# A two-layer decoder trunk: which use of a mixer weight stores its high part, and where small constants are loaded

## The chip, the cores and the metric

The kernel runs on one core of a Trainium2 chip. The metric is the time of one execution on the device in microseconds; lower is better. The engines are TensorE (PE; its weight loads are listed as PEld), VectorE (DVE), ScalarE (ACT), GpSimd (POOL) and SyncE (SP), which issues the transfers; 16 DMA engines carry them between DRAM and the on-chip memory.

## The reference

A trunk of two layers runs over 1040 tokens (16 meta tokens and 1024 real ones) of width 1024. In each layer a mixer projects the normalised input, attends in three ways (sliding window, stick breaking, gated linear) and projects back; a PEER feed-forward network then picks 16 of 4096 experts for each of eight heads. Cut to what matters:

```python
for i in range(DEPTH):                                  # DEPTH = 2
    h = h + hybrid_mixer(rms_norm(h, attn_norm[i]), w_in[i], ..., w_out[i])
    h = h + peer_ffn(rms_norm(h, ffn_norm[i]), peer_w_q[i], peer_sub_keys[i], peer_u[i], peer_v[i])
return rms_norm(h[:, BLOCK:], final_norm)

def hybrid_mixer(xn, w_in, ..., w_out):
    proj = xn @ w_in                                    # 1024 x 2320
    ...                                                 # three kinds of attention
    return mixed @ w_out                                # 1024 x 1024
```

## The kernel before

**Numbers in two parts.** Matrix products in float32 are made from numbers cut into a high and a low part: TensorE multiplies high by high, high by low and low by high. For a weight, `wload` brings a piece of 128x512 floats (256 KB) into one of four raw buffers, and `split` writes the high part with ScalarE (line 274) and the low part as raw minus high, here half on GpSimd and half on VectorE (line 281).

**Quarters.** The mixer takes the tokens in four quarters (272, 256, 256 and 256 tokens). For each quarter `proj_span` makes 18 groups of `dense` (36 pieces of `w_in`, called `a0_...` and `a1_...` for the two layers), attention follows, and `out_span` makes 8 groups of `dense` (16 pieces of `w_out`, `o0_...`, `o1_...`). All matmuls of `dense` are line 335: 12 for each piece. So each piece of a mixer weight is used four times in its layer, once for each quarter.

**Kept parts.** At the first use of a piece `wpiece` splits the raw weights and `keep` (line 293) writes the parts to DRAM. Mixer weights ask for both parts (`both=True`), other weights for the low one alone. A later use finds the name in `kept` and loads the low part (line 311), and the high part either from DRAM (line 310) or, where it was not kept, by loading the raw piece and making the high part anew with one ScalarE copy (line 308). The parts land in two rings of five buffers, `whi` and `wlo`, the raw pieces in the ring of four, `wraw`. The rings are handed out in program order. `make_m`, which builds a table for the feed-forward network between attention and projection, uses the `wraw` ring too: four pieces a call, three calls after the first quarter's attention.

**Order.** The program order is: normalise the first quarter, load the small constants (`load_constants`, seven transfers), load the second quarter's activations for their squares (`first(1)`, eight transfers), then project the first quarter. Within a layer the projection of quarter q+1 stands between the attention and the output projection of quarter q. A scheduler turns the program into one fixed list for each engine, by priority in program order and by its own estimate of when operands are ready, so attention of one quarter and the projection of the next lie interleaved. At run time each engine's list stays as it is. Engine tasks depend on each other by semaphores that the framework places.

In the second layer the first quarter is projected between the two halves of the first layer's last expert product (`values`, matmuls of line 1203).

Of the kernel before, what the change touches and what calls it, by code (L numbers as in the profile page):

```python
# [59 lines left out]
def tile_trunk(ctx, tc, h0, w_pk, wgate, w2, glab, w_out, wqT, keysT, u_pk, v_w, sinks,  # L60
# [104 lines left out]
    def ps1(tag="a"):  # L165
        r = rings[tag]
        r[1] += 1
        return banks[r[0][(r[1] - 1) % len(r[0])]]
# [57 lines left out]
    def load_constants():  # L226
        SP.dma_start(w2s[0:16], w2.rearrange("l r c -> r l c"))
        SP.dma_start(w2s[16:32], w2.rearrange("l r c -> r l c"))
        SP.dma_start(glab_sb, glab)
        SP.dma_start(g_mix, n_mix)  # L230
        SP.dma_start(sink_b, sinks.rearrange("l h -> (l h)").unsqueeze(0).to_broadcast([128, 16]).rearrange(
            "p (l h) -> p l h", l=DEPTH))
        SP.dma_start(g_ffn, n_ffn)
        SP.dma_start(g_fin, n_fin)
# [48 lines left out]
    def wload(src):  # L283
        raw = sb([128, 512], F32, "wraw")
        SP.dma_start(raw, src)
        return raw

    kept = {}

    def keep(name, part):  # L290

        t = dram.tile([128, 512], F32, name=name, tag=name)
        SP.dma_start(t, part.bitcast(F32))
        return t

    def wpiece(src, key=None, both=False):


        hi = sb([128, 512], F32R, "whi")
        lo = sb([128, 512], F32R, "wlo")  # L300
        if key not in kept:
            split(wload(src), hi, lo)
            if key is not None:
                kept[key] = (keep(f"{key}h", hi) if both else None, keep(f"{key}l", lo))
            return hi, lo
        kh, kl = kept[key]
        if kh is None:
            ACT.activation(hi, wload(src), AF.Copy)  # L308
        else:
            SP.dma_start(hi.bitcast(F32), kh)  # L310
        SP.dma_start(lo.bitcast(F32), kl)
        return hi, lo
# [26 lines left out]
    def rstd(ver, sp, sqk=None):  # L339

        acc = sqs[ver]
        ss = ps1("d")
        n = len(sp.tiles)
        if sqk:
            PE.matmul(ss[:, 0:8], zb, identb[:, 0:8], start=True, stop=False)
            for sq in sqk:
                for j, (o, m) in enumerate(sp.tiles):
                    PE.matmul(ss[0:m, j:j + 1], sq[:, o:o + m], ones[:, 0:1], start=False, stop=False)
            PE.matmul(ss[:, 0:8], zb, identb[:, 0:8], start=False, stop=True)
        else:  # L350
            for j, (o, m) in enumerate(sp.tiles):
                PE.matmul(ss[0:m, j:j + 1], acc[:, sp.c0 + o:sp.c0 + o + m], ones[:, 0:1], start=True, stop=True)
        ms = sb([128, 8], F32, "nms")
        rs = sb([128, 8], F32, "nrs")
        grp = [(0, 1, META), (1, n, 128)] if sp.meta else [(0, n, 128)]
        for a, b, m in grp:
            DVE.tensor_scalar(ms[0:m, a:b], ss[0:m, a:b], 1.0 / D, EPS, op0=ALU.mult, op1=ALU.add)
            POOL.tensor_tensor(rs[0:m, a:b], ms[0:m, a:b], mhalf[0:m, a:b], op=ALU.pow)
        ps = ps1("d")
        for j, (o, m) in enumerate(sp.tiles):  # L360
            PE.matmul(ps[:, o:o + m], rs[0:m, j:j + 1].to_broadcast([m, 128]), ident[0:m, 0:m], start=True, stop=True)
        rb = sb([128, 272], F32, "rb")
        ACT.activation(rb[:, 0:sp.w], ps[:, 0:sp.w], AF.Copy)
        return rb

    def apply(ver, sp, g, x, rb, ks=range(KT), src=None, buf="ht"):

        w = sp.w
        for k in ks:
            xt = sb([128, 272], F32, buf)  # L370
            if src is None:
                SP.dma_start(xt[:, 0:w], hv[ver][k][:, sp.c0:sp.c1])
            DVE.scalar_tensor_tensor(xt[:, 0:w], xt[:, 0:w] if src is None else src[:, k], g[:, k:k + 1], rb[:, 0:w],
                                     op0=ALU.mult, op1=ALU.mult)
            xh = x.at(0, k, 0, w)
            ACT.activation(xh, xt[:, 0:w], AF.Copy)
            DVE.tensor_tensor(x.at(1, k, 0, w), xt[:, 0:w], xh.bitcast(F32), op=ALU.subtract)
# [45 lines left out]
    def proj_span(l, L, sp, x):  # L423

        A = Layer()
        w = sp.w
        A.sp = sp
        A.mo = mo = META if sp.meta else 0
        A.b0 = b0 = (sp.c0 + mo - META) // 128
        def proj(g):  # L430
            return dense(w_pk[l, g], x, sp, f"a{l}_{g}")

        def vtrans(g, dst, col, base, pad):
            pss = proj(g)
            st = sb([128, 384], F32, "vst", 2)
            off = 0
            if pad:
                off = 112
                if sp.meta:
                    POOL.memset(st[:, 0:112], 0.0)  # L440
            evac(st[:, off:off + w], pss, sp)
            tp = ps1("d")
            for j in range(2):
                PE.transpose(tp[:, j * 128:(j + 1) * 128], st[:, off + mo + j * 128:off + mo + j * 128 + 128], ident)
            if sp.meta:
                if pad:
                    PE.transpose(tp[:, 256:384], st[:, 0:128], ident)
                    DVE.tensor_copy(dst[:, base - 1, col:col + 128], tp[:, 256:384])
                else:
                    PE.transpose(tp[0:16, 256:384], st[:, 0:16], ident)  # L450
                    DVE.tensor_copy(dst[0:16, 0, col:col + 128], tp[0:16, 256:384])
            DVE.tensor_copy(dst[:, base:base + 2, col:col + 128],
                            tp[:, 0:256].rearrange("p (b c) -> p b c", b=2))

        pr = str((b0 // 2) % 2)
        A.qaT = sb([128, 4, 272], F32, "qaT" + pr)
        A.qbT = sb([128, 2, 272], F32, "qbT" + pr)
        A.qcT = sb([128, 272], F32, "qcT" + pr)
        A.kcT = sb([128, 272], F32, "kcT" + pr)
        A.cum = cum = sb([128, 272], F32, "cum" + pr)  # L460
        A.gr = sb([128, 2, 272], F32, "gr" + pr)
        A.vc = sb([128, 3, 256], F32, "vc" + pr)
        for i in range(2):
            evac(L.kbT[:, i, sp.c0:sp.c1], proj(i), sp)
        for i in range(2):
            evac(A.qbT[:, i], proj(2 + i), sp, scale=0.125)
        for i in range(2):
            vtrans(4 + i, L.vb, 128 * i, b0 + 1, False)
        yield A
        if sp.meta:  # L470
            POOL.memset(L.kaT[:, slot(-1) * 128:slot(-1) * 128 + 112], 0.0)
        evac(L.kaT[:, slot(b0) * 128 - mo:slot(b0) * 128 - mo + w], proj(6), sp)
        vtrans(7, L.va, 0, slot(b0), True)
        for i in range(4):
            evac(A.qaT[:, i], proj(8 + i), sp, scale=0.125)
        evac(A.kcT, proj(12), sp)
        evac(A.qcT, proj(13), sp, scale=32.0 ** -0.5)

        graw = sb([128, KT, 16], F32, "graw")
        SP.dma_start(graw, wgate[l])  # L480
        ghl = sb([128, KT, 32], F32R, "ghl")
        ACT.activation(ghl[:, :, 0:16], graw, AF.Copy)
        DVE.tensor_tensor(ghl[:, :, 16:32], graw, ghl[:, :, 0:16].bitcast(F32), op=ALU.subtract)
        ps = ps1("d")
        for k in range(KT):
            PE.matmul(ps[0:32, 0:w], ghl[:, k, :], x.at(0, k, 0, w), start=(k == 0), stop=False)
            PE.matmul(ps[0:16, 0:w], ghl[:, k, 0:16], x.at(1, k, 0, w), start=False, stop=(k == KT - 1))
        A.gl = sb([32, 272], F32, "gl" + pr)
        ACT.activation(A.gl[:, 0:w], ps[0:32, 0:w], AF.Copy)
        for i in range(2):  # L490
            vtrans(14 + i, A.vc, 128 * i, 1, False)
        for i in range(2):
            pss = proj(16 + i)
            evac(A.gr[:, i], pss, sp)
        yield A
# [739 lines left out]
    quarters = [Span(0, 272), Span(272, 528), Span(528, 784), Span(784, 1040)]  # L1235
# [5 lines left out]
    XR = [Rows((HA, HB)), Rows((HC, HA)), Rows((HB, HC)), Rows((HA, HB))]  # L1241
# [14 lines left out]
        make_m(0, i)  # L1256
    L = attn_layer(0)
    apply(0, quarters[0], g_attn[:, 0], XR[0], rstd(0, quarters[0], sqk), src=hq)
    load_constants()
    first(1)  # L1260
    pr = proj_span(0, L, quarters[0], XR[0])
    A = next(pr)
    rb = rstd(0, quarters[1])
    apply(0, quarters[1], g_attn[:, 0], XR[1], rb, range(4))
    next(pr)
# [1 line left out]
    for l in range(DEPTH):  # L1267
# [10 lines left out]
        for q in range(4):  # L1278
# [25 lines left out]
            if q < 3:  # L1304
                A = nA
# [53 lines left out]
        if more:  # L1359
            values(l, Q, G, (0, 1), 0)  # L1360
            L = attn_layer(l + 1)
            pr = proj_span(l + 1, L, quarters[0], XR[0])
            A = next(pr)
# [80 lines left out]
```

## Time and profile before

| | |
|---|---|
| runs before, median (lowest to highest) | 3353.25 us (3343.89 to 3354.38), 3 runs |
| profiled execution, time | 3348.59 us |
| profiled execution, span | 3346.8 us |
| mean granted clock of TensorE | 0.959 |
| TensorE matmuls, busy | 3139.3 us, 94% |
| VectorE, ScalarE, GpSimd, busy | 62%, 39%, 29% |
| moved by DMA | 655.56 MB, 195 GB/s over the span |

The profile comes from one execution. Busy times are sums over instructions; a matmul's end is modelled, so a busy TensorE isn't TensorE at its peak, and the mean time of one matmul tells more. "Idle before, releaser" is the time in which an engine waited and what ended it. The granted clock is given as a share of full speed.

### The profile page before, as it was taken

The page shows a single profiled execution, that of the slowest core. Times are in us where ns is not written, and L with a number is a line of the kernel's source. Part 1 is how long each engine was busy: PE and PEld are TensorE (multiplying, and loading weights), DVE is VectorE, ACT ScalarE, POOL GpSimd, SP SyncE. Part 2 cuts the span into 40 slices and gives each one's busy share as a digit, 9 for nine tenths or more (in the row PEclk, how much of TensorE's full clock was granted, in tenths as well). Part 3 has the DMA queues.
Part 4 walks back from the last instruction along what each step waited for, and adds up shares of the span by engine and source line. Part 5 has one row for each costly group of instructions (what it writes and reads, how often), then busy time and mean ns, then how long its engine had stood idle before and what let it go on. Part 6 is the DMA issues. An engine that isn't in the chain of part 4 may idle for free.

```text
span 3346.8 us, 65733 instructions
## 1 busy us (share of the span) xinstructions
PE 3139.3 (94%) x23453; PEld 2636.6 (79%) x23453; DVE 2074.0 (62%) x6694; ACT 1311.1 (39%) x3013; POOL 958.4 (29%) x976
## 2 busy tenths in 40 slices
PE   7999999988999988999898999999889999899998
PEld 7686887768999987888874878877668888688788
DVE  4546446689885389753225464457796835986457
ACT  4534334424334343324344343344333344343354
POOL 4314021313454341010401131213244524301135
PEclk9899998989999999999997999999799999999999
DMA  8767774736346555446964677757454466554665
GB/s 292 235 194 251 248 258 136 215 127 236 128 137 191 182 174 172 157 145 200 333 232 141 211 263 241 251 161 238 149 181 148 154 191 219 172 179 143 195 191 169
DMA packets 406442, 655.56 MB, mean 196 GB/s; under 512 B 44560, under 2 KB 122464, under 8 KB 406112
## 3 DMA queue, kind: packets, MB, share of 16 engines
q1 hardware_dynamic: 406112, 651.35, 60.3%
q8 instruction: 184, 3.01, 0.4%
q14 instruction: 146, 1.20, 0.1%
HBM read 492.70 MB, written 158.47 MB: 195 GB/s over the span
## 4 chain that ended last, share of the span: by engine, by line
PE 67%; DVE 20%; DMA 7%; ACT 2%; issue 2%; SPq 1%; POOL 1%; DVEq 0%; POOLq 0%; ACTq 0%
PE b L1113 18%; PE b L1203 15%; PE b L335 13%; PE b L1164 4%; PE b L987 3%; PE b L703 2%; DVE arena_r L1197 2%; DMA arena<-h 2%; DVE arena L998 2%; DVE arena L1000 2%; DVE arena L997 2%; PE b L618 2%; PE b L757 2%; DMA arena<-in_w_pk_dram 1%; DVE arena L999 1%
## 5 line engine op out<-in xcount | busy, mean ns | idle before, releaser
L281 POOL TENSOR_TENSOR arena_r<-arena,arena_r 128x512 fp32r<-128x512 f32 (+1 forms) x440 | 555.4, 1268 | 869.5 <-ACT arena_r L274 800.3
L1113 PE MATMUL b<-arena_r 128*128 128x512 f32 (+2 forms) x3840 | 763.0, 357 | 17.5 <-DVE arena L261 15.5
L1203 PE MATMUL b<-arena_r 128*128 128x512 f32 (+2 forms) x4224 | 749.7, 337 | 31.4 <-DVE arena_r L1197 24.6
L1203 PEld LDWEIGHTS b<-arena_r 128*128 128x128 f32 x4224 | 643.8, 190 | 126.2 <-DVE arena_r L1197 35.7
L335 PE MATMUL b<-arena_r 128*128 128x256 f32 (+1 forms) x4992 | 702.6, 295 | 36.4 <-ACT arena_r L274 10.0
L1113 PEld LDWEIGHTS b<-arena_r 128*128 128x128 f32 x3840 | 626.0, 191 | 115.6 <-DVE arena L261 16.2
L335 PEld LDWEIGHTS b<-arena_r 128*128 128x128 f32 x4992 | 643.9, 196 | 76.3 <-issue 19.7
L274 ACT ACTIVATE arena_r<-arena 128x512 fp32r<-128x512 f32 x456 | 285.1, 629 | 479.8 <-PE b L1113 104.1
L1197 DVE TENSOR_TENSOR arena_r<-arena,arena_r 128x512 fp32r<-128x512 f32 (+2 forms) x352 | 270.8, 783 | 314.6 <-ACT arena_r L1196 313.5
L308 ACT ACTIVATE arena_r<-arena 128x512 fp32r<-128x512 f32 x288 | 181.2, 631 | 384.3 <-PE b L1203 120.9
L987 PE MATMUL b<-arena_r 128*128 128x256 f32 (+1 forms) x1632 | 208.9, 283 | 3.4 <-DMA arena_r<-m_3l 1.8
L987 PEld LDWEIGHTS b<-arena_r 128*128 128x128 f32 (+1 forms) x1632 | 196.5, 183 | 13.5 <-issue 4.4
L1152 DVE TENSOR_TENSOR arena<-arena 128x2048 f16<-128x2048 f16 x129 | 176.1, 1367 | 45.3 <-PE b L1164 45.3
L257 POOL TENSOR_TENSOR arena<-arena 128x256 f32<-128x256 f32 (+1 forms) x126 | 107.9, 856 | 315.1 <-ACT arena L256 312.4
L1120 POOL TENSOR_TENSOR arena<-arena 128x32 f32<-128x32 f32 (+25 forms) x91 | 98.5, 1089 | 305.4 <-ACT arena L1171 206.6
L1196 ACT ACTIVATE arena_r<-arena 128x512 fp32r<-128x512 f32 (+2 forms) x352 | 172.2, 502 | 31.1 <-PE b L1203 27.6
L1164 PEld LDWEIGHTS <-arena 128*128 128x128 f16 x4128 | 144.4, 118 | 17.2 <-issue 14.4
L1169 DVE SCALAR_TENSOR_TENSOR arena<-b,arena 128x224 f32<-128x224 f32 (+20 forms) x129 | 63.1, 499 | 145.9 <-PE b L1164 145.7
L1164 PE MATMUL b<-arena 128*128 128x32 f16 x4128 | 152.3, 190 | 0.0
L715 DVE TENSOR_TENSOR_SCAN arena<-arena,zf 128x384 f32<-128x384 f32 (+6 forms) x116 | 104.1, 900 | 76.5 <-ACT arena L710 75.5
L421 ACT ACTIVATE arena<-b 128x256 f32<-128x256 f32 (+1 forms) x144 | 55.2, 384 | 211.7 <-PE b L335 211.2
L1157 DVE TENSOR_TENSOR arena<-arena 128x1024 f16<-128x1024 f16 x129 | 123.3, 956 | 0.1
(267 smaller groups left out, 3796.7 us busy)
## 6 DMA issues: line engine op xcount, KB each, us to landing
arena<-in_v_w_dram SPq DMA_DIRECT2D x288, 256.0 KB, 2.9
arena<-in_u_pk_dram SPq DMA_DIRECT2D x256, 256.0 KB, 3.0
arena_r<-a_0h SPq DMA_DIRECT2D x108, 256.0 KB, 3.7
arena_r<-a_0l SPq DMA_DIRECT2D x108, 256.0 KB, 3.9
arena_r<-a_1h SPq DMA_DIRECT2D x108, 256.0 KB, 3.2
arena_r<-a_1l SPq DMA_DIRECT2D x108, 256.0 KB, 3.5
arena<-m SPq DMA_DIRECT2D x96, 256.0 KB, 4.5
arena<-h SPq DMA_DIRECT2D x192, 128.0 KB, 3.1
```

The costliest lines, as they stand in the source:

```text
L274: ACT.activation(hi, src, AF.Copy)
L281: e.tensor_tensor(lo[:, a:b], src[:, a:b], hi[:, a:b].bitcast(F32), op=ALU.subtract)
L308: ACT.activation(hi, wload(src), AF.Copy)
L335: PE.matmul(ps, wt[:, ks], x.at(low, k, xo, sp.w), start=(k == 0 and i == 0), stop=(k == KT - 1 and i == 2))
L987: PE.matmul(ps, yv(half, low, k, o, m), wt[:, kk * 256:kk * 256 + 256], start=(k == 0 and i == 0 and e == 0), stop=(k == KT - 1 and i == 2 ...
L1113: PE.matmul(ps, wt[:, ks], yv(h, low, k, 0, w // 2 if h is None else w), start=(k == 0 and i == 0), stop=(k == KT - 1 and i == 2))
L1152: DVE.tensor_tensor(Lh, iotaM.unsqueeze(1).to_broadcast([128, 4, 128, 4]), v4(P.mT[half], 128), op=ALU.is_equal)
L1157: DVE.tensor_tensor(R, R0.unsqueeze(2).to_broadcast([128, 4, 2, 32, 4]), P.gg[half][:, t0 // 4:t0 // 4 + 4].unsqueeze(3).to_broadcast([128 ...
L1164: PE.matmul(ps[:, i * 32:(i + 1) * 32], Lh[:, b, :, t], R[:, b, part, :, t], start=(part == 0), stop=(part == 1))
L1196: ACT.activation(ah, G[:, r, o:o + w], AF.Copy)
L1197: last = DVE.tensor_tensor(al, G[:, r, o:o + w], ah.bitcast(F32), op=ALU.subtract)
L1203: PE.matmul(ps, wt[:, d * 128:d * 128 + 128], pr[low], start=(opens and r == 0 and i == 0), stop=(closes and r == 31 and i == 2))
```

## The change

Of the two parts of a mixer weight only the low one is now written to DRAM at the first use. At the second use the raw piece is loaded again, its high part is made by a ScalarE copy and written to DRAM then; third and fourth use load both parts as before. Apart from that, the small constants and the second quarter's activations are now loaded after the first six groups of the first quarter's projection (`next(pr)` runs it up to its first `yield`) in program order, no longer ahead of them.

```diff
@@ wpiece
         if key not in kept:
             split(wload(src), hi, lo)
             if key is not None:
-                kept[key] = (keep(f"{key}h", hi) if both else None, keep(f"{key}l", lo))
+                kept[key] = [None, keep(f"{key}l", lo)]
             return hi, lo
         kh, kl = kept[key]
         if kh is None:
             ACT.activation(hi, wload(src), AF.Copy)
+            if both:
+                kept[key][0] = keep(f"{key}h", hi)
         else:
             SP.dma_start(hi.bitcast(F32), kh)
         SP.dma_start(lo.bitcast(F32), kl)
@@ the main program
     apply(0, quarters[0], g_attn[:, 0], XR[0], rstd(0, quarters[0], sqk), src=hq)
+    pr = proj_span(0, L, quarters[0], XR[0])
+    A = next(pr)
     load_constants()
     first(1)
-    pr = proj_span(0, L, quarters[0], XR[0])
-    A = next(pr)
     rb = rstd(0, quarters[1])
```

## Rows read from the trace of the kernel before

**Rows 1.** The page, busy time of the engines (first part).

```profile
PE 3139.3 (94%) x23453; PEld 2636.6 (79%) x23453; DVE 2074.0 (62%) x6694; ACT 1311.1 (39%) x3013; POOL 958.4 (29%) x976
```

**Rows 2.** Busy time by stretch; the first column after the colon is the length.

```profile
core 0: us, PE busy (x) PEld busy (x) DVE busy (x) ACT busy (x) POOL busy (x), PEclk, DMA share, GB/s
8.00:107.60 99.60, 82.00 (x533) 74.43 (x531) 47.80 (x128) 44.76 (x108) 41.97 (x62) 0.91 0.92 311
107.60:150.00 42.40, 38.32 (x236) 22.31 (x237) 23.58 (x72) 21.93 (x78) 17.49 (x19) 0.72 0.59 188
150.00:245.00 95.00, 94.66 (x760) 76.58 (x758) 45.47 (x109) 37.28 (x107) 14.79 (x20) 1.00 0.65 200
260.00:300.00 40.00, 36.95 (x294) 30.14 (x293) 26.10 (x57) 20.76 (x62) 21.14 (x21) 1.00 0.96 324
...
400.00:440.00 40.00, 39.51 (x307) 35.10 (x307) 22.15 (x63) 16.01 (x50) 7.97 (x9) 1.00 0.86 287
1604.00:1682.30 78.30, 66.82 (x471) 61.90 (x469) 20.60 (x46) 30.11 (x64) 37.94 (x40) 0.96 1.01 358
1670.00:1680.00 10.00, 8.92 (x66) 8.01 (x64) 2.66 (x8) 3.47 (x7) 3.76 (x4) 1.00 1.04 386
1682.30:1760.00 77.70, 77.17 (x331) 61.02 (x332) 22.39 (x35) 35.37 (x65) 2.67 (x19) 1.00 0.64 213
1840.00:1915.00 75.00, 73.51 (x594) 61.57 (x595) 30.58 (x72) 23.81 (x68) 8.56 (x12) 1.00 0.68 220
...
2068.00:2110.00 42.00, 41.51 (x324) 36.97 (x324) 23.48 (x67) 18.09 (x52) 7.58 (x8) 1.00 0.86 286
```

**Rows 3.** The same stretches, line 335 alone: PE, PEld, PEclk, DMA share, GB/s.

```profile
8.00:107.60 99.60, 65.23 (x411) 61.09 (x411) 0.91 0.92 311
107.60:150.00 42.40, 4.20 (x22) 3.44 (x22) 0.72 0.59 188
...
260.00:300.00 40.00, 23.30 (x165) 21.04 (x163) 1.00 0.96 324
363.00:375.00 12.00, 11.14 (x92) 10.98 (x93) 1.00 0.84 267
...
1604.00:1682.30 78.30, 58.31 (x414) 55.31 (x414) 0.96 1.01 358
```

**Rows 4.** What PE waited for, 8 to 110 us: total us, times, longest.

```profile
PE b L335 <- ACT arena_r L274: 3.3, 5, 1.4
PE b L335 <- POOL arena_r L281: 3.3, 4, 2.0
```

**Rows 5.** The same, 1590 to 1690 us.

```profile
PE b L335 <- ACT arena_r L274: 4.2, 2, 3.1
PE b L444 <- ACT arena L421: 3.8, 5, 1.7
PE b L335 <- POOL arena_r L281: 1.6, 4, 0.5
```

**Rows 6.** Busy time by stretch, line 274 on ScalarE alone.

```profile
8.00:107.60 99.60, 21.99 (x36) 0.91 0.92 311
```

**Rows 7.** Timeline of the start: start, length, engine, line, what, idle before.

```profile
5.03 0.43 SPq L227 DMA_DIRECT2D w2s<-in_w_dram  x1
...
8.35 1.85 SPq L285 DMA_DIRECT2D arena<-in_w_pk_dram  x4
...
14.33 3.30 DVE L281 TENSOR_TENSOR arena_r<-arena,arena_r 128x256 fp32r<-128x256 f32 x2 [1.16 <-ACT arena_r L274]
...
15.59 0.40 ACT L363 ACTIVATE arena<-b 128x272 f32<-128x272 f32 x1 [0.26 <-PE b L361]
...
17.75 1.31 DVE L373 SCALAR_TENSOR_TENSOR arena<-arena,g_attn 128x272 f32<-128x272 f32 x3
```

**Rows 8.** What SP's queue waited for, 100 to 250 us.

```profile
SPq L310 <- PE b L335: 48.8, 30, 4.3
```

**Rows 9.** What ScalarE waited for, 8 to 110 us.

```profile
ACT arena_r L274 <- DMA arena<-in_w_pk_dram: 11.5, 11, 4.1
```

## The prediction

> **What bounds the kernel now.** I read the page first. TensorE is busy in 94% of the span [rows 1], so an edit can only earn what TensorE idles or works slowly for, and must be looked at stage by stage. Next I asked for the busy times by stretch. In two stretches the DMA engines are full while TensorE has gaps: the first use of the projection weights in the first layer (8 to 107.6 us: DMA share 0.92, 311 GB/s, PE 82.0 of 99.6 us) and in the second (1604 to 1682.3 us: share 1.01, 358 GB/s, PE 66.82 of 78.3) [rows 2]. In the second uses it is the other way round: 150 to 245 us has PE at 94.66 of 95 and DMA at 200 GB/s, 1840 to 1915 us PE at 73.51 of 75 and 220 GB/s [rows 2]. The same stretches for line 335 alone show that its matmuls take longer where the weights are late: 65.23/411 = 159 ns in the first layer's first use and 58.31/414 = 141 ns in the second's, against 11.14/92 = 121 ns where they are there in time (363 to 375 us) [rows 3]. The waits say who is late: PE stands behind the split weights, on ScalarE and GpSimd, for 3.3 + 3.3 us in the first stretch and 4.2 + 1.6 in the other [rows 4, 5].
>
> **The change: what moves.** A piece is 128x512 floats, 0.262 MB. At its first use it now causes 0.79 MB of traffic (raw in, high and low out), afterwards 0.52. At its second use it causes 0.52 MB (high and low in), afterwards 0.79 (raw and low in, high out) and one more ScalarE copy of 21.99/36 = 0.61 us [rows 6]. There are 36 pieces of w_in and 16 of w_out in each layer, so 104 writes (27.3 MB) move and 104 copies are new (63 us of ScalarE, which is idle more than half of its time in every second-use stretch [rows 2]). The total of bytes stays.
>
> **Gains at the first uses.** First layer, w_in: PE has 99.6 - 82.0 = 17.6 us idle, and line 335 is (159 - 121) ns x 411 = 15.5 us slower than it need be. Of the idle time 6.6 us is waiting for weights; the other 11 us are not the change's to give. So at most 33.1 - 11 = 22 us, at least the 6.6. DMA would allow more: 99.6 x 311 = 31.0 MB, less 36 x 0.262 = 9.4 MB, is 21.5 MB, or 69 us at the same rate. But a piece of pure projection takes 12 x 121 ns = 1.45 us and then wants 0.52 MB, 361 GB/s, which is about what DMA gives at full share (358, at best 386 in 10 us) [rows 2]: weights come just in time, not ahead. I take 15, two thirds of the way to the upper end. What follows, 107.6 to 150 us, is short of work at a granted clock of 0.72 and DMA share 0.59 [rows 2], a chain of small attention steps that starts when the projection ends and simply moves forward.
> Second layer, w_in: idle 11.5 us, 5.8 of it for weights, line 335 slow by 20 ns x 414 = 8.2: at most 14, at least 5.8; I take 11, since the share of 1.01 leaves no doubt of the cause. Behind it stand matmuls of line 1203 with PE at 77.17 of 77.7 us and 213 GB/s [rows 2], which pass the gain on.
> w_out, first layer, 260 to 300 us: share 0.96; line 335 at 23.30/165 = 141 ns gives 3.3 us, idle is 3.1 us [rows 2, 3]. No single row of waiting proves it, so 0 to 6.4; I take 3, and 3 for the twin in the second layer.
> Start: the seven small loads go out from 5.03 us, and the first weights behind them at 8.35. VectorE splits weights from 14.33 for 3.3 us, and so begins to normalise at 17.75 although its factor was ready at 15.59 + 0.40 [rows 7]. Weights 3.3 us earlier free VectorE: 0 to 1.8 us, I take 1.5. The 8 loads of the second quarter's activations, moved back with them, are wanted after the first projection only.
> Sum of the gains: 15 + 11 + 3 + 3 + 1.5 = 33.5 us (12 to 51).
>
> **Costs at the second uses.** First layer, w_in (150 to 245 us): 19.0 MB + 9.4 = 28.4 MB in 95 us, 299 GB/s, under what DMA has shown; ScalarE 37.3 + 22.0 = 59.3 of 95. SP stood 48.8 us in 30 waits until PE gave a weight buffer free [rows 8], so loads run ahead of PE and cover most of it: low end 0. High end: all writes laid bare, 9.4 MB at 358 GB/s, 26 us. The nearest row is the first use itself, where ScalarE stood 11.5 us in front of these very pieces until the raw ones landed [rows 9] and PE lost 6.6: I take 5. Second layer (1840 to 1915): 16.5 MB + 28.4 pieces x 0.262 = 23.9 MB in 75 us, 319 GB/s: 0 to 21, I take 6.
> w_out at its second use: 400 to 440 us moves 287 x 40 = 11.5 MB, with 16 writes 15.7; at 358 GB/s that needs 43.8 us, 3.8 too many. In 2068 to 2110 it is 12.0 + 4.2 = 16.2 MB, 45.3 us, 3.3 too many [rows 2]. I take 4 and 3 (0 to 12 each, all 4.2 MB bare). Here the ceiling decides. At the best 10 us rate of 386 the two cost 1 us together. The Trainium skill (HBM Reference, Specifications) puts a core that streams alone at about 425 GB/s; no stretch here shows that, and by it these two costs would be nothing and the forecast 7 us lower.
> The four raw-weight buffers now serve, in program order, twelve pieces for make_m and then the second quarter's projection. Of the 22 matmuls of line 335 between 107.6 and 150 us [rows 3] some 16 run ahead of that today; pushed behind it they cost 16 x 121 ns: 2 us.
> Sum of the costs: 5 + 6 + 4 + 3 + 2 = 20 us (2 to 73). Net: -13.5 us. The profiled execution took 3348.59 us with its 1.8 us around the span, so 3335; it lies 4.7 under the median of 3353.25, so in terms of the runs 3340 us.
>
> **Rivals.**
> *Slower: the wait for a weight buffer goes over to ScalarE.* Today it is SP that stands until PE frees a buffer, and nothing of attention is behind it. Afterwards the copy writes that buffer, so ScalarE stands, with the exponentials, tanh and evacuations of attention queued behind it, and PE waits for those. The price: 48.8/30 = 1.6 us a wait [rows 8]. If a third of it reaches PE at each of the 104 copies, that is 56 us, and with gains of 33.5 the kernel ends 22 above the median, 3375. It decides from (33.5 + 10)/104 = 0.42 us a copy. Against it: the same copies wait for the same buffers in the first use, and there PE is held up by late weights, not by attention [rows 4, 5]. The Trainium skill (TensorE: Matmul & The Clock Gate, Architectural detail) says that ScalarE and VectorE are strict first in, first out, while TensorE can pull weight loads forward; no row here shows that order by itself, and by that rule this rival stands as told. Chance 0.15.
> *No change: the first uses aren't that DMA-bound.* Only the named waits go, 6.6 + 5.8 us, for what else PE idles on is evacuations (line 444, 3.8 us [rows 5]) and splits; against costs of about 11 that is nothing: 3352. For it: GpSimd's share of the splits stays as it is. Against it: the DMA share of 1.01 [rows 2]. Chance 0.23.
> *More: the second uses hide everything.* Then only the 2 us of make_m remain: -31.5, 3322. For it the 48.8 us that SP waits for PE; against it the 392 GB/s that w_out would want. Chance 0.14.
>
> **How the numbers follow.** The forecast, 3330 to 3350, has 0.48. About 0.3%, 10 us, is what a measurement of this kernel can tell from no change: under 3343 is faster, over 3363 slower. Faster: 0.14, most of the forecast's 0.48 (0.41), a little of the no-change case: 0.56. Same: 0.07 + 0.22: 0.29. Slower: 0.15. The range leaves out the slower rival and the far end of the best case: 3318 to 3360.
>
> **What the next profile would show.** Right: the first use of w_in ends near 92 us instead of 107.6, with PE's waits behind lines 274 and 281 down; the second layer's takes about 67 us instead of 78 and DMA there falls under a share of 1.0; 104 new copies of 0.61 us; DMA near 300 GB/s in the second uses with PE still at 97% or more. Wrong: PE gaps in the second uses with ScalarE or the new copy's line as releaser, or first-use stretches that keep their length although DMA moves a third less.

## The result, and the profile after

The changed kernel took 3305.62 us (median of 4 runs, 3304.01 to 3306.66) beside 3349.61 us for the kernel before: ratio 0.9869, 95% interval 0.985 to 0.9888, 44 us faster. The forecast was 13.5 us faster, with 3318 us as the lower end of its range. Run again, the changed kernel came to 0.985 (0.9828 to 0.9871).

The busy times of the page, to be held against [rows 1]: the span is 44.5 us shorter, of which TensorE's busy time gives 15.9 and its idle time the other 28.6; ScalarE has the 104 copies more.

```profile
PE 3123.4 (95%) x23453; PEld 2629.0 (80%) x23453; DVE 2068.4 (63%) x6694; ACT 1367.3 (41%) x3117; POOL 960.6 (29%) x976
```

**The first use.** What TensorE waited for in the changed kernel, 8 to 110 us, and then in the second layer's first use with the expert product behind it, 1572 to 1757 us (line 337 is what line 335 was, the matmuls of the projections). The waits of [rows 4] and [rows 5] for split weights are gone; in the second layer the wait of the transposes (line 446, formerly 444) for ScalarE's evacuations, its copies of TensorE's results, has grown from 3.8 to 5.2 us.

```profile
PE b L363 <- POOL arena L360: 2.1, 1, 2.1
PE b L337 <- ACT arena_r L378: 2.0, 1, 2.0
...
PE b L446 <- ACT arena L423: 5.2, 4, 3.2
PE b L620 <- DVE arena L261: 3.8, 1, 3.8
```

**The start.** The timeline, beside [rows 7]: the first weights go out 3.3 us earlier, but VectorE begins to normalise only 0.9 us earlier. It now begins as soon as its factor is ready, but the factor itself comes 0.8 us later (16.37 + 0.38 us, before 15.59 + 0.40).

```profile
5.04 1.86 SPq L285 DMA_DIRECT2D arena<-in_w_pk_dram  x4
...
16.37 0.38 ACT L365 ACTIVATE arena<-b 128x272 f32<-128x272 f32 x1
...
16.84 1.79 DVE L375 SCALAR_TENSOR_TENSOR arena<-arena,g_attn 128x272 f32<-128x272 f32 x3
```

**Stage by stage.** The mixer's stages can be cut at marks that every variant has, read off the timeline of SP's transfers: the last write of a low part of w_in ends the first quarter's projection, the 36th load of a low part the second's, and the last write of `h` in each burst an output projection (in the second layer the first burst stands for the projection of its first quarter with the expert product behind it). Where the timeline lists the last two writes of a burst as one row, the middle of that row is the mark; so the border between `q2` and `q3` lies up to 2.6 us ahead of the last write itself, and by that write the two stages of the changed kernel are 8.6 and 6.8 us shorter in the first layer and 3.0 and 10.7 in the second, with the same sums. `w_in` stands for an input projection, `w_out` for an output projection, `q0` to `q3` for the quarters. The table is made from these marks and the spans: length of a stage in the kernel before, and how much longer (+) or shorter (-) it is in a variant, in us. "again" is the second profile of the changed kernel; the experiments follow below.

```
stage               before   after   again   e3_gain  e4_cost  e9_double  e10_o2  e13_copy  e14_write  e11_o4
w_in, q0             109.6   -21.4   -23.4    -20.8     +0.1     -0.1      -0.9     +1.1      +3.1      -0.3
w_in, q1             130.3    +6.0    +3.2     +2.1     +2.9    +15.7      +1.0     +1.0      +0.6      +1.0
w_out, q0             58.1   -10.0    -7.1     -6.3     +1.2     +7.8      +1.5     -0.8      +0.4      +1.7
w_out, q1            146.1   +16.1   +16.1     +8.9     +7.3    +16.8     +10.0     -0.4     +13.9      +1.9
w_out, q2            159.7    -7.6    -7.3     -1.8     -5.5    -13.9      -6.5     -1.1     -11.2      -2.1
w_out, q3            162.1    -7.7    -8.0     +1.8     -8.1    -16.2      -7.6     +2.0      -7.8      +3.3
feed-forward         855.9    -1.0    -0.8     -3.2     +1.9     -0.1      +1.6     +1.0      +3.8      +0.6
2nd layer w_in, q0   164.2    -3.1    -5.1     -5.2     +0.2     +0.4      +1.3     -2.1      +4.5      +1.4
w_in, q1             131.0    -0.8    -4.1    -10.7     +1.8    +13.3       0.0     -4.3      -5.5      -7.0
w_out, q0             54.9    -3.5    -2.6     -7.5     -4.3     +5.8      -0.9     +1.0      -1.0      +0.4
w_out, q1            142.4    +6.3    +9.1     -0.9     +8.2    +11.6     +10.7     -2.2     +15.6      -3.6
w_out, q2            151.4    -2.6    -2.6     +1.5     -0.7     -8.8      -0.4     +6.1      -0.9      +0.4
w_out, q3            152.3   -11.2   -11.5     +0.3    -11.6    -12.1      -9.3     +3.1      -8.6      +1.9
feed-forward         929.1    -3.9    -4.5     -1.2     -0.9     -1.3      +0.9     -4.9      -6.5      +5.7
sum of the span     3346.8   -44.5   -48.6    -43.0     -7.6    +19.0      +1.4     -0.4      +0.5      +5.3
```

Three things are to be seen. The first uses (`q0`) are shorter. The second uses (`q1`) are longer in three of four cases, in the first layer's output stage of the second quarter (the long stage, below) by 16 us. And the last two quarters of each layer, whose data flow is the same as before, are shorter by 15 us in the first layer and 14 in the second. Two executions of one program differ by up to 3.3 us in a stage ("after" and "again"), so single entries below that say nothing. Between variants the scatter is larger: stages that an edit doesn't touch differ by up to 7.0 us from the kernel before (second layer's `w_in, q1` in e11_o4).

**What the long stage does.** Busy time by stretch, of the kernel before: the output stages of quarters 1, 2 and 3, and the last quarter's of the second layer; under them line 335 alone in the first three.

```profile
297.90:444.00 146.10, 140.73 (x1082) 114.58 (x1082) 62.76 (x156) 55.41 (x142) 27.90 (x42) 0.96 0.77 250
444.00:603.70 159.70, 152.91 (x1139) 121.71 (x1131) 82.17 (x185) 59.08 (x153) 28.99 (x42) 0.95 0.57 179
603.70:765.80 162.10, 142.55 (x1031) 106.00 (x1031) 133.32 (x704) 60.81 (x131) 39.98 (x51) 0.91 0.56 175
2265.50:2417.70 152.20, 132.62 (x913) 99.94 (x911) 116.76 (x555) 58.00 (x126) 42.69 (x50) 0.84 0.57 181
...
297.90:444.00 146.10, 80.97 (x624) 75.67 (x624) 0.96 0.77 250
444.00:603.70 159.70, 86.50 (x614) 77.77 (x614) 0.95 0.57 179
603.70:765.80 162.10, 31.01 (x203) 27.99 (x202) 0.91 0.56 175
```

The same of the changed kernel, with the first use (0 to 88.2 us) ahead:

```profile
0.00:88.20 88.20, 75.45 (x524) 70.49 (x525) 41.64 (x122) 45.15 (x105) 49.08 (x90) 0.96 0.81 261
272.50:434.70 162.20, 154.71 (x1198) 123.18 (x1196) 79.28 (x189) 75.25 (x199) 33.40 (x46) 0.95 0.73 237
434.70:586.80 152.10, 148.35 (x1121) 117.72 (x1120) 79.61 (x180) 56.38 (x147) 27.36 (x40) 0.98 0.61 193
586.80:741.10 154.30, 134.47 (x983) 102.14 (x982) 130.15 (x696) 58.56 (x119) 37.19 (x50) 0.93 0.59 185
...
2236.10:2377.20 141.10, 127.09 (x892) 96.28 (x891) 113.82 (x550) 55.71 (x117) 34.68 (x48) 0.89 0.61 196
...
272.50:434.70 162.20, 84.44 (x636) 77.66 (x636) 0.95 0.73 237
434.70:586.80 152.10, 82.62 (x609) 74.60 (x608) 0.98 0.61 193
586.80:741.10 154.30, 28.53 (x201) 25.77 (x199) 0.93 0.59 185
```

All matmuls less those of the projections are attention and its like: 1082 - 624 = 458 in the long stage before, 1198 - 636 = 562 after, 104 more. In the two stages that follow there are 525 + 828 before and 512 + 782 after, 59 fewer (some of the rest had lain ahead of the long stage). The long stage isn't longer because TensorE stands (7.5 us idle, before 5.4), but because it does work there that came earlier or later before.

Which work lies in a stage is fixed before the run: in two executions of the changed kernel the matmuls start in the same order (23449 of 23453 places agree), and each edit has another list. Counted in that order, 1317 matmuls of other lines lie ahead of the 1680th matmul of the projections (three input and two output projections) in the kernel before, and 1358 in the changed one; ahead of the 1056th (two input projections and one output projection) it is 876 and 779. So of the surplus between these two places 41 matmuls came later before, and 97 came earlier: the shorter first stages leave attention over, and the long stage takes it.

### The profile page after: what moved, and what is told of

Read it like the earlier page. It is cut to its first block, busy times and chain, and to the rows that moved or that the text cites. A ratio compares the mean times of both kernels' runs of the same rounds, so it can differ in the third digit from the quotient of the medians.

```text
span 3302.3 us, 65898 instructions
## 1 busy us (share of the span) xinstructions
PE 3123.4 (95%) x23453; PEld 2629.0 (80%) x23453; DVE 2068.4 (63%) x6694; ACT 1367.3 (41%) x3117; POOL 960.6 (29%) x976
## 4 chain that ended last, share of the span: by engine, by line
PE 34%; DVE 10%; DMA 3%; issue 1%; ACT 1%; POOL 1%; SPq 0%; POOLq 0%; DVEq 0%; ACTq 0%
PE b L1115 9%; PE b L1205 9%; PE b L337 6%; PE b L1166 2%; PE b L989 1%; PE b L705 1%; DMA arena<-h 1%; DVE arena_r L1199 1%; DVE arena L1000 1%; PE b L759 1%; DVE arena L999 1%; PE b L620 1%; DVE arena L1002 1%; DMA arena<-in_v_w_dram 1%; POOL arena_r L281 1%
## 5 line engine op out<-in xcount | busy, mean ns | idle before, releaser
L281 POOL TENSOR_TENSOR arena_r<-arena,arena_r 128x512 fp32r<-128x512 f32 (+1 forms) x440 | 566.4, 1292 | 848.3 <-ACT arena_r L274 783.0
L1115 PE MATMUL b<-arena_r 128*128 128x512 f32 (+2 forms) x3840 | 764.8, 358 | 16.1 <-DVE arena L261 14.0
L337 PE MATMUL b<-arena_r 128*128 128x256 f32 (+1 forms) x4992 | 690.9, 293 | 25.5 <-DVE arena L359 8.1
L274 ACT ACTIVATE arena_r<-arena 128x512 fp32r<-128x512 f32 x456 | 286.2, 630 | 494.3 <-PE b L1115 115.8
L308 ACT ACTIVATE arena_r<-arena 128x512 fp32r<-128x512 f32 x392 | 246.0, 630 | 431.1 <-PE b L1205 122.8
L989 PE MATMUL b<-arena_r 128*128 128x256 f32 (+1 forms) x1632 | 210.5, 284 | 2.9 <-DMA arena_r<-m_0l 2.1
L1198 ACT ACTIVATE arena_r<-arena 128x512 fp32r<-128x512 f32 (+2 forms) x352 | 172.2, 502 | 24.5 <-PE b L1205 20.9
L717 DVE TENSOR_TENSOR_SCAN arena<-arena,zf 128x272 f32<-128x272 f32 (+6 forms) x116 | 105.1, 909 | 58.9 <-ACT arena L712 57.7
L281 DVE TENSOR_TENSOR arena_r<-arena,arena_r 128x256 fp32r<-128x256 f32 (+1 forms) x140 | 78.4, 563 | 94.0 <-ACT arena_r L274 82.3
L578 POOL TENSOR_TENSOR arena<-arena,mhalf 128x8 f32<-128x8 f32 (+3 forms) x43 | 60.2, 1399 | 221.4 <-DVE arena L575 154.4
```

The lines of the kernel that those rows point to most:

```text
L274: ACT.activation(hi, src, AF.Copy)
L281: e.tensor_tensor(lo[:, a:b], src[:, a:b], hi[:, a:b].bitcast(F32), op=ALU.subtract)
L337: PE.matmul(ps, wt[:, ks], x.at(low, k, xo, sp.w), start=(k == 0 and i == 0), stop=(k == KT - 1 and i == 2))
L989: PE.matmul(ps, yv(half, low, k, o, m), wt[:, kk * 256:kk * 256 + 256], start=(k == 0 and i == 0 and e == 0), stop=(k == KT - 1 and i == 2 ...
L1115: PE.matmul(ps, wt[:, ks], yv(h, low, k, 0, w // 2 if h is None else w), start=(k == 0 and i == 0), stop=(k == KT - 1 and i == 2))
L1198: ACT.activation(ah, G[:, r, o:o + w], AF.Copy)
```

## The experiments

The theories: **1**, the forecast's account with its sizes corrected: the first uses gain, the second uses cost, the sum is the result. **2**, the second uses' cost is given back, because attention of the next quarter fills TensorE meanwhile. **3**, a rival: the moved constants carry the surplus. **4**, a rival: any other fixed order of the engines' lists would be worth as much.

**e1_consts and e2_kept: the two edits apart.** Each is one hunk of the diff alone.

> Only the moved loads of constants and activations; the kept parts as in the kernel before. The forecast's own account: the start is 1.5 us shorter and nothing else changes, 3348 us beside 3350. Rival A, that the move carries what was under-forecast (the first weights reach the chip sooner and with them the whole first quarter): 25 to 30 us faster, near 3322. Rival B, that a new fixed order of the engines' lists is worth several us by itself, up or down: anywhere within 10 us of 3350, and the trace differs in later quarters that the edit doesn't touch.

> Only the kept parts, constants loaded where they were. The forecast's own account with its terms resized: nearly the whole gain, 40 to 43 us, 3307 to 3310. Rival A (the move of the constants carries it): 12 to 18 us, about 3335. If both edits are needed together, less than either sum.

Measured: the constants alone 0.9945 (0.9928 to 0.9962), 18 us faster; the kept parts alone 0.9869 (0.984 to 0.9898), 45 us, as much as both edits. So with the kept parts changed the move adds nothing that can be measured, and theory 3 falls for the changed kernel. Alone, the move fits none of the three expectations: it shortens the first projection by 7.0 us, not by 1.5, and where the other 11 us lie the stages don't settle: no other is as much as 5 us shorter.

**e3_gain and e4_cost: the gain without the cost, and the cost without the gain.**

```diff
# e3_gain, first use
-                kept[key] = (keep(f"{key}h", hi) if both else None, keep(f"{key}l", lo))
+                kl = keep(f"{key}l", lo)
+                kept[key] = (kl if both else None, kl)
# e4_cost, first and second use
+                kept[key] = [None, keep(f"{key}l", lo), keep(f"{key}h", hi) if both else None]
...
+            ACT.activation(hi, wload(src), AF.Copy)
+            if both:
+                kept[key][0] = keep(f"{key}g", hi)
```

In the two expectations that follow, "theory 1" is what is called theory 2 above: no cost at the second uses.

> The gain of the first uses without the cost of the second: the first use writes the low part alone, and every later use loads that low part for the high one too, so the high part is never made anew or written and the result is not the reference's. Theory 1 (the second use costs nothing, the first uses are worth more than forecast): as fast as the changed kernel, 3303 to 3309. The forecast as sized: 20 us faster than the changed kernel, near 3286, as its costs are gone. Constants stay where they were.

> The cost of the second uses without the gain of the first: the first use writes both parts as in the kernel before, the second loads the raw piece, makes the high part with a ScalarE copy and writes it once more to another place, and the later uses load that. 27 MB more written than before. Forecast as sized: 20 us slower, near 3370. Theory 1: no slower, 3347 to 3353. The rival in which ScalarE stands for weight buffers: 40 us and more slower.

Measured: the gain alone 0.9861 (0.9837 to 0.9885), 44 us; the cost alone 0.9972 (0.9958 to 0.9986), 7 us faster than before. The first is the time of the changed kernel without any of its second-use work, so what the first uses no longer write carries the whole result, and 27 MB more of writes and 104 copies don't slow the kernel at all. That they make it 7 us faster was not expected, and no run says why; their other list may be worth that much. Theory 1 falls with it: no cost stands at the end. Yet in the table e4_cost's second-use stages are longer, by 2.9, 7.3, 1.8 and 8.2 us, and its last quarters shorter, by 13.6 and 12.3; e3_gain, with nothing at the second use, has last quarters as long as before. But its long stage is 8.9 us longer, too: 1164 - 624 = 540 attention matmuls lie in it, 82 more than before, and they came from ahead (769 lie ahead of the 1056th projection matmul, not 876; 1313, nearly the 1317 of before, ahead of the 1680th). So part of the 16.1 us of the changed kernel is no cost of the second use. Busy time by stretch of e3_gain, the long stage and the two that follow, to be held against those of the kernel before (1082, 1139 and 1031 matmuls), and the projections (line 336) of the long stage:

```profile
273.00:428.00 155.00, 149.02 (x1164) 120.72 (x1165) 77.90 (x184) 63.80 (x173) 32.19 (x44) 0.96 0.71 235
428.00:585.90 157.90, 152.90 (x1148) 121.51 (x1145) 82.67 (x186) 58.90 (x153) 28.77 (x42) 0.96 0.58 182
585.90:749.80 163.90, 143.65 (x1032) 107.60 (x1031) 132.10 (x704) 60.01 (x131) 39.72 (x51) 0.90 0.56 174
...
273.00:428.00 155.00, 81.84 (x624) 75.90 (x624) 0.96 0.71 235
```

**e5_win and e6_wout: the kept edit for one kind of weight.** The edit of e2_kept holds for names that begin with "a" or with "o" only.

> The kept edit for the projection weights (w_in, 72 of the 104 pieces) alone, constants where they were. By the theory that the gain is the shortened first use of w_in and that no cost remains at the end: 33 to 38 us faster, 3311 to 3316. By the forecast as sized (26 gained, 11 paid, 2 for the raw buffers): 13 us, 3336.

> The kept edit for the output weights (w_out, 32 of the 104 pieces) alone. By the forecast (6 gained, 7 paid): no change, 3349. By the theory that costs at the second use are given back before the mixer ends: 5 to 9 us faster, 3340 to 3344; the stage of the second quarter's output projection is longer by some 8 us all the same, and the third and fourth quarters shorter.

Measured: 0.9927 (0.9911 to 0.9944), 25 us, and 0.999 (0.9978 to 1.0002), 5 us that can't be told from nothing. Together they are 30, the joint edit is 45; the parts don't add up, and e5_win is 8 us short of what theory 2 expected of it. In e6_wout the first output stages are 7.7 and 5.7 us shorter and the second ones 20.9 and 9.0 longer, and the third and fourth quarters give 13.9 and 7.5 back.

**e7_low2: the low parts later, too.** First use: no write; second use: split again, both parts written.

```diff
-                kept[key] = [None, keep(f"{key}l", lo)]
+                kept[key] = [None, None if both else keep(f"{key}l", lo)]
...
+        if kl is None:
+            split(wload(src), hi, lo)
+            kept[key] = [keep(f"{key}h", hi), keep(f"{key}l", lo)]
+            return hi, lo
```

> The changed kernel, and its low parts of mixer weights too are kept at the second use only: the first use writes nothing, the second loads the raw piece, splits it anew and writes both. If DMA still binds the changed kernel's first uses, they shorten again by some 5 us in the first layer and 5 in the second and the kernel takes about 3295. If TensorE's own work binds them by now (no wait for weights is left among its waits there): the same time as the changed kernel, 3305, and the added splits cost nothing.

Measured: 0.9881 (0.9863 to 0.9898), 3311 us: not faster than the changed kernel, and 5 and 11 us above its two medians (3305.62 and 3299.95), with intervals that overlap. The stage marks of the table need the low parts' writes, which this kernel doesn't have there; busy time by stretch to the end of the first projection and from there on, of the kernel before (first projection alone), of the changed kernel and of e7_low2, tells it instead:

```profile
0.00:114.50 114.50, 94.01 (x586) 83.00 (x586) 55.75 (x158) 50.27 (x125) 50.36 (x91) 0.91 0.90 305
```

```profile
0.00:96.60 96.60, 83.68 (x582) 77.61 (x582) 48.98 (x155) 50.37 (x125) 49.27 (x90) 0.96 0.79 253
96.60:250.00 153.40, 149.22 (x1133) 115.73 (x1133) 85.03 (x223) 89.62 (x239) 42.08 (x47) 0.93 0.78 257
```

```profile
0.00:96.60 96.60, 84.16 (x582) 78.25 (x584) 52.39 (x155) 49.48 (x126) 48.18 (x90) 0.96 0.51 147
96.60:250.00 153.40, 141.35 (x1064) 107.92 (x1063) 99.80 (x235) 83.75 (x231) 68.14 (x79) 0.91 0.73 241
```

With 10.2 MB less to move in the first stretch (253 - 147 GB/s, over 96.6 us), TensorE does the same 582 matmuls in it: transfers no longer set the first projection of the changed kernel, so there was nothing left to gain there. What follows is worse: 69 matmuls fewer in the next 153 us, VectorE 15 us busier with the second split, and the first output stage ends at 279.6 us, where the changed kernel's ends at 272.5 and the kernel before's at 297.9.

**e8_nohi: no high part kept at all.** The changed kernel without the two lines that keep the high part.

> The changed kernel with the high parts never kept: the second, third and fourth use all load the raw piece and copy it. 27 MB less written, 208 copies of 0.63 us more on ScalarE. If the second uses' writes cost the changed kernel anything at its end: 5 to 10 us faster than it, 3296 to 3300. If that cost is given back anyway and copies are free: 3305. If ScalarE's queue, standing for weight buffers, holds attention up: slower than it by 10 us or more, 3315 and up.

Measured: 0.9952 (0.9935 to 0.9968), 3335 us, 29 us slower than the changed kernel though it writes 27 MB less. What ScalarE's copies (line 308) waited for where matmuls of the projections ended the wait, first e8_nohi and then the changed kernel:

```profile
ACT arena_r L308 <- PE b L335: 160.1, 151, 3.5
...
ACT arena_r L308 <- PE b L337: 31.6, 29, 4.1
```

This is the slower rival's wait: ScalarE stands for buffers that TensorE hasn't freed, 160 us in all. TensorE's idle time isn't longer for it (3328.5 - 3149.1 = 179.4 us; 178.9 in the changed kernel), its busy time is (3149.1 against 3123.4, at a mean granted clock of 0.957 against 0.965), and the last quarters give nothing back. The ratio of the busy times, 1.008, is that of the two clocks, so the same matmuls ran at a lower granted clock. The list, too, is nearly back at that of the kernel before (1318 ahead of the 1680th, not 1358). That the waits cause the loss was not isolated.

**e9_double: the suspected cost doubled.** e4_cost with a second copy of the high part written at the second use (`keep(f"{key}i", hi)`).

> The kernel of e4_cost with the suspected cost doubled: at the second use the high part is written twice (a second copy that nobody reads), so 55 MB more are written than by the kernel before. If the cost of the second use is given back before the mixer ends, because attention of the next quarter fills TensorE meanwhile: at most 5 us slower than e4_cost, 3341 to 3347, still not slower than the kernel before. By the forecast's terms scaled (18 for one write): 36 us slower than before, 3385.

Measured: 1.0049 (1.0032 to 1.0066), 16 us slower than before and 23 slower than e4_cost: my expectation missed. The second-use stages, with the first output stages between them, take 40.3 us more in the first layer and 30.7 in the second; 30.1 and 20.9 come back. So the cover is bounded: with two writes a piece more is lost than comes back.

**e10_o2 and e11_o4: w_out's cost at the second and at the fourth use.** First use as before; a count of the uses picks where the copy and the extra write go.

```diff
+        again = both and key[0] == "o" and uses[key] == 2        # e11_o4: 4
-        if kh is None:
+        if kh is None or again:
             ACT.activation(hi, wload(src), AF.Copy)
+            if again:
+                keep(f"{key}g", hi)
```

> For w_out alone and without any gain: the first use keeps both parts as before, the second use loads the raw piece, copies it and writes the high part once more. Theory (given back): the stage of the second quarter's output projection is 7 us or more longer, the third and fourth quarter shorter by about as much, and the end within 5 us of the kernel before, 3345 to 3355. Forecast as sized: 7 us slower.

> The same copies and writes for w_out, at the fourth use and not the second, where no attention is left to fill TensorE and DMA already has a share of 0.94 (736 to 766 us). Theory (the second use is free only because of what fills it): not given back, 4.2 MB at about 350 GB/s a layer, so 10 to 24 us slower than the kernel before and than e10_o2, 3360 to 3374. If what counts is the luck of another list: no systematic difference from e10_o2.

Measured: 0.9976 (0.9962 to 0.9991), 8 us faster (more than expected), and 0.9998 (0.9985 to 1.001), no change (the execution profiled for e10_o2 was one of its longer ones, 3350 us). Stages of e10_o2, then its projections alone (line 340):

```profile
299.60:455.70 156.10, 149.95 (x1152) 120.72 (x1151) 70.82 (x170) 69.01 (x175) 32.80 (x45) 0.96 0.78 256
455.70:608.90 153.20, 149.81 (x1095) 118.75 (x1095) 77.53 (x178) 56.05 (x147) 26.36 (x40) 0.96 0.59 192
608.90:763.30 154.40, 134.65 (x1003) 103.20 (x1003) 129.60 (x696) 58.25 (x120) 37.41 (x50) 0.93 0.59 186
...
299.60:455.70 156.10, 83.39 (x636) 77.44 (x636) 0.96 0.78 256
455.70:608.90 153.20, 84.24 (x604) 76.33 (x605) 0.96 0.59 192
608.90:763.30 154.40, 28.90 (x202) 26.06 (x201) 0.93 0.59 186
```

This is the cleanest case, since all ahead of the long stage is as before: 1152 - 636 = 516 attention matmuls in it, 58 more than before; 491 and 801 in the two that follow, 34 and 27 fewer. The long stage takes 10.0 us more, of which 9.2 is TensorE's busy time for 70 matmuls more, and the two that follow 14.1 less. At the fourth use nothing is moved (1317 ahead of the 1680th, as before), and the last output stages of the two layers are 3.3 and 1.9 us longer, within the scatter; my expectation of 10 to 24 us missed. So a write isn't free only where attention can take its place. That the last stage's 20 us of idle TensorE hide it is argued, not shown.

**e13_copy and e14_write: the copy alone, the write alone.** e10_o2 without its `keep`, and e10_o2 with the kept part loaded as before and written again.

> e10_o2 without its write: the first use of w_out keeps both parts as before, the second loads the raw piece and copies it (32 ScalarE copies in all, no byte more moved than before), later uses load the kept part. If the shift of attention into the second quarter's output stage comes from the write's load on DMA: no shift, stages as in the kernel before, 3349 to 3352. If it comes from the copies and the raw buffers in the engines' lists: the shift of e10_o2 (50 to 60 matmuls, some 10 us to and fro) and its time, 3341 to 3345.

> e10_o2 without its copy: the second use of w_out loads both kept parts as before and writes the high part once more. If the write brings the shift of attention: as e10_o2, 50 to 60 matmuls moved into the second quarter's output stage, given back by the fourth quarter, 3341 to 3345. If the copies bring it: no shift, and the write is hidden or costs up to 7 us, 3350 to 3357.

Measured: 0.9984 (0.9973 to 0.9995) and 0.9987 (0.9973 to 1.0001), 5 us faster, and 3 that can't be told from nothing; the time of e14_write fits neither of its expectations, so the stages have to tell. The long stage of e13_copy and its line 338, then that of e14_write and its line 340:

```profile
299.30:445.00 145.70, 139.39 (x1077) 114.23 (x1077) 62.77 (x156) 64.52 (x160) 28.45 (x42) 0.96 0.77 250
...
299.30:445.00 145.70, 81.30 (x632) 76.54 (x633) 0.96 0.77 250
...
302.00:462.10 160.10, 152.33 (x1142) 121.86 (x1141) 71.42 (x171) 59.88 (x158) 32.20 (x45) 0.95 0.78 252
...
302.00:462.10 160.10, 84.83 (x625) 77.88 (x625) 0.95 0.78 252
```

With the copy alone 445 attention matmuls lie in the stage, as before (458), and nothing comes back later. With the write alone there are 517, the stage is 13.9 us longer, and the next two are 19.0 shorter. So the write moves the attention work forward, not the copy. It does so in the list, as the order of the matmuls shows: ahead of the 1680th projection matmul lie 1317 others in the kernel before, 1304 in e13_copy, 1394 in e14_write, 1358 in e10_o2 and e4_cost, and 1398 in e9_double. The scheduler, with the write in the program, orders the work differently; what the write's transfers do in the run itself isn't separated from that, for no variant has the write with the list of before. Theory 4 falls in its general form: e13_copy and e11_o4 have other lists too, and shift next to nothing. In a narrower form, that another list is worth some us by itself, it stands untested.

**e12_again: the changed kernel once more,** to see how far the stages of two executions differ.

> The changed kernel once more, on this chip and with a second profile, to tell how far the stages of two executions of one program differ: its time 3300 to 3308, and the marks between stages within 3 us of those of its first profile.

Measured: 3299.95 us, ratio 0.985. Column "again" of the table: no stage differs from "after" by more than 3.3 us, and the rise and return of each layer are there again (+16.1, then -7.3 and -8.0; +9.1, then -2.6 and -11.5).

## Why the prediction was wrong

**The step that failed** is "Costs at the second uses": I read each as a loss at the end, 20 us in sum. Alone (e4_cost) they make the kernel 7 us faster, not 20 slower. As sizes of stages they weren't far off: forecast 5, 6, 4 and 3, with 2 for make_m, which no run isolates; the stages of e4_cost are 2.9, 1.8, 7.3 and 8.2 us longer, 20.2 in sum. (In the changed kernel it is 6.0, -0.8, 16.1 and 6.3, but part of that is attention left over by the shorter first stages, as in e3_gain.) What was missing is what the third and fourth quarters give back, 25.9 us in e4_cost and 29 in the changed kernel (29.4 again). I took the order of TensorE's work as given and priced the write by DMA alone. But the list is another one with the write in it: attention of the next quarter comes earlier in it, so the stage is longer for the work that it holds, and that work is missing later. e4_cost shows the whole cost as no loss, e10_o2 the exchange nearly matmul for matmul (58 more, then 61 fewer), e14_write that the write alone brings it about, e9_double that it has an end. That the same work had been dearer in the last stages, where TensorE stood 19.6 us and ran at a granted clock of 0.91 and 0.84, is argued: in the changed kernel the clock there is 0.93 and 0.89, but the first layer's last stage has as much idle time (19.8 us).

This step is 20 of the 30.5 us between forecast and result: with the costs at nothing the forecast would have been 33.5 us faster instead of 13.5. The other 10 are gains taken too small.

**The gains** were 33.5 us forecast (15, 11, 3, 3 and 1.5); the table has 38.0 in those stages, 38.2 again, and e3_gain's time 44. By that time they were 10 us too small in sum; singly they were mis-sized both ways. The 15 for the first layer's projection is called two thirds of the way to the upper end, but is two thirds of 22; two thirds of the way from 6.6 would be 17. That projection gave 21.4 with the start, not 16.5, of which its successor takes up to 6.0 back, since part of its work moved there; by the same 582 to 586 matmuls it is some 18 us; the first output stage 10.0 and 7.1, not 3. The second layer's projection gave 3.1 and 5.1, not 11: the waits for weights are gone as forecast, but TensorE now waits longer for evacuations (5.2 us, 3.8 before), and 11 us of idle time are left in that stage (14 before).

**The start** was mis-sized little in the changed kernel (0.9 us where I took 1.5), and too small where nothing else is changed (7.0 in e1_consts).

**The rivals.** "More" was the nearest to what happened, but it too left the gains at their sizes and knew nothing of a return; that its reason (loads run ahead of TensorE) is what hid the writes no run shows. "Slower", ScalarE standing for buffers, is a real wait in the changed kernel (31.6 us in 29 waits), and e4_cost, with the same copies at the same place, is no slower; e8_nohi shows it at 160 us beside a loss of 29. The Trainium skill (TensorE: Matmul & The Clock Gate, Architectural detail) states that ScalarE works strictly first in, first out; no run here tested that by itself. "No change" is refuted by e3_gain.

**The ceiling of DMA** that decided the costs of w_out was there. Over the whole of those stages the changed kernel moved 237 and 262 GB/s, but in 400 to 440 us it runs at a DMA share of 1.02 with 356 GB/s, as I had feared. TensorE stays busy all the same: it does 53 matmuls fewer of the projections and 62 more of the rest than the kernel before does in those 40 us. All matmuls and the projections' of the changed kernel, then the projections' of the kernel before (the rest of it is in [rows 2]):

```profile
400.00:440.00 40.00, 38.60 (x316) 31.70 (x314) 21.70 (x51) 20.03 (x55) 12.79 (x13) 1.00 1.02 356
...
400.00:440.00 40.00, 24.09 (x177) 21.51 (x175) 1.00 1.02 356
...
400.00:440.00 40.00, 29.50 (x230) 27.77 (x230) 1.00 0.86 287
```

The figure of the Trainium skill (HBM Reference, Specifications) that I set beside it, about 425 GB/s for a core that streams alone, stays unseen here: the highest rate in the rows is 386 GB/s over 10 us [rows 2].

**Of what the next profile was to show,** the first use ends at 88.2 us (forecast 92), the waits behind the splits are gone, and TensorE keeps 97% in the second projection (132.45 of 136.3 us). The second layer's stage was to be 11 us shorter and wasn't, though DMA's share in it fell from 1.01 (1604 to 1682.3 us) to 0.81 (1572 to 1656.9 us).

**What stays open:** why e1_consts is 18 us faster and not 7; why e4_cost and e10_o2 are 7 and 8 us faster than the kernel before, with nothing but cost added; how much of the second uses' cost the list hides and how much would have been hidden anyway; why the two kinds of weight together are worth some 15 us more than apart; and by which of attention's steps e8_nohi loses. No variant is measurably better than the changed kernel; e2_kept is its equal.

## What to carry to other kernels

Where one engine runs a list in which two jobs lie interleaved, a longer stage isn't by itself a loss: count the work that it holds before pricing it, and follow the lead to the end of the last stage that the jobs share. Price a moved transfer twice, in the stage that it leaves and in the one that it enters, and ask there what else the busiest engine has to do, and whether the list of its work will still be the same. And try gain and cost apart: a kernel with only the cost tells whether there is one.

## What the hardware showed that was not expected

The limit that transfers set to a stage lay between two shares not far apart. In the first projection a DMA share of 0.90 with 305 GB/s (kernel before, to 114.5 us) went with waits for weights and some 18 us more for the same work; a share of 0.79 with 253 GB/s (changed kernel) was no hindrance any more, since 0.51 with 147 GB/s (e7_low2) gave the same 582 matmuls in the same 96.6 us. Nor did a full DMA always hold TensorE up: at a share of 1.02 it was busy 38.6 of 40 us (changed kernel, 400 to 440 us), for other work lay in its list. And the idle time of an engine that stands for buffers can be large without an idle TensorE beside it: 160.1 us of ScalarE in e8_nohi, 31.6 us in the changed kernel, with 179.4 and 178.9 us of idle TensorE.
